# Gate and up products with head and rest of the tokens side by side in 512 columns, in a two-layer decoder trunk

## The chip, the core and the metric

The kernel runs on one core of a Trainium2 chip. The metric is the device time of one execution in microseconds, the median of three runs. The engines that matter: TensorE (PE in the profile), which multiplies and writes its sums into PSUM, eight banks of 512 fp32 columns in 128 partitions; VectorE (DVE) and ScalarE (ACT), which read PSUM and work on SBUF; SP and POOL (GpSimd), which issue the loads of the weights.

## The reference

Two residual layers on 512 tokens of 1024 features, in fp32. The first mixes tokens by causal pooling windows, the second by dilated sliding-window attention; after each mixer comes a SwiGLU feed-forward, and a last norm ends it. The change touches the feed-forward alone:

```python
D_FF = -(-8 * D_MODEL // (3 * 256)) * 256      # 2816
...
def swiglu(h, w_gate, w_up, w_down):
    g = jnp.einsum('bsd,df->bsf', h, w_gate)
    u = jnp.einsum('bsd,df->bsf', h, w_up)
    return jnp.einsum('bsf,fd->bsd', jax.nn.silu(g) * u, w_down)
...
    for i in range(DEPTH):
        ...
        h = rmsnorm(x, norm_ffn[i])
        x = x + swiglu(h, ffn_w_gate[i], ffn_w_up[i], ffn_w_down[i])
```

## The kernel before

**Heads and rests.** Every fp32 operand of a product is split into two parts: a head (`hi`, the value cast to the format fp32r, by ACT, line 139 for weights) and a rest (`lo`, value minus head, by DVE, line 143). A product is then three matmuls into one PSUM sum: head times head, weights' head times tokens' rest, weights' rest times tokens' head. Each matmul loads its own 128x128 stationary tile.

**Seven products for eight.** In the feed-forward the weights and tokens are cut into two-by-two blocks, and seven block products do the work of eight. Their operands are sums and differences of blocks; for the weights these are formed by loads that add (POOL, line 107) and by DVE (line 145), for the tokens before the first group.

**Groups.** `ffn` (line 537) works through 11 groups of 256 of the 2816 inner features. A group is seven products, `Group.product` (line 614), numbered 0 to 6. Each runs over gate and up (`g`), four chunks of 128 input features and the three matmuls (lines 623 to 628): 24 matmuls of 256 columns (half of the tokens) per product. The sums collect in three one-bank tensors: p takes products 0, 2, 4, 6, r takes 1 and 5, q takes 3. After each product `done` (line 632) reads them: `keep` is a copy of p after product 0 (line 636), `ct` gets copies of r and p after 1 and 2 (638, 640), then DVE sums after 3, 4, 5 (642, 644, 646), silu and the multiplication by up (647 to 650, 653 and 658). `first_half` and `second_half` build the seven token operands `u` of the down products and split them.

**Down.** After group 3, 6 and 9 a down stage (`down`, line 696) multiplies the `u` of three groups by seven combinations of the down weights: for each, two halves of 128 tokens, three groups, three matmuls of 512 columns (line 712), and after each half DVE adds the sum to or takes it from the stream x (719, 721). It uses p, r and q too, two banks of each; here q takes product 3 from zero, and product 0's p is added to x by itself. Groups 9 and 10 go through a last stage without the seven products.

**Order.** PE runs in program order (`manual_schedule`); the instructions of the other engines are ordered by the framework's scheduler, which obeys priorities: the readers of sums are marked `URGENT` (2000), those after products 5 and 6 have 100. The weights of all products stand in one list in the order of use (`FFN_ORDER`, line 47, filled by `enqueue_ffn`); `weights` (line 118) loads up to ten entries ahead and splits up to four ahead. A ring of five tiles holds split weights, another of five the raw ones, and three more (`vraw`) those that are formed by adding. The first weight's raw tile is kept until it has been added to the second's.

**PSUM.** Four banks belong to the pool `mm` (q, and other stages), four to `ffps` (two tensors each of p and r).

Of the kernel before, what the change touches and what calls it, by code (L numbers as in the profile page):

```python
# [17 lines left out]
P = 128  # L18
S = 512
# [27 lines left out]
FFN_ORDER = (  # L47
    [("two", 0)] + [("quad", n) for n in (2, 3)] + [("down", 0)]
    + [("quad", n) for n in (4, 5, 6)] + [("down", 1)] + [("quad", n) for n in (7, 8, 9)] + [("down", 2)]
    + [("quad", 10)] + [("last", 3)]  # L50
)

TWO = [(g, i) for g in (0, 1) for i in (0, 3)] + [(g, i) for i in (1, 2, 4, 5, 6) for g in (0, 1)]
# [5 lines left out]
def trunk_kernel(ctx: ExitStack, tc: tile.TileContext, x_in, xT, gam, gains, consts, ident_d, w0, wT, w1, wv, w_down, out):  # L59
# [15 lines left out]
    mm = ctx.enter_context(tc.tile_pool(name="mm", bufs=4, space=bass.MemoryType.PSUM))  # L75
# [92 lines left out]
    def enqueue_ffn(layer):  # L168
# [27 lines left out]
        def down(b):  # L196
            pairs = BLOCKS[b]
            at = layer * (NF // 2) + pairs[0]
            dn[b] = [{}, {}]
            for i in range(7):  # L200
                for js, a, n in zip(dn[b], (at, at + 2), (2, len(pairs) - 2)):
                    operand(js, i, lambda m, k: tiles[k, :, a : a + n, COLS[m]], (n, S), 10)

        for step, n in FFN_ORDER:
            if step == "two":
                for g, i in TWO:
                    quad(n + g, i, 5)
            elif step == "quad":
                for i in range(7):
                    quad(n, i)  # L210
            elif step == "down":
                down(n)
            else:
                dn[n] = [rows_of(w_down)(layer * NF + 2 * pair, half) for pair in BLOCKS[n] for half in range(2)]
# [27 lines left out]
    h_both = [stat.tile([P, NC * S + 2 * SHIFT], F32R, name=f"h_{part}") for part in ("hi", "lo")]  # L242

    def tokens_at(shift):
        return [h[:, shift : shift + NC * S].rearrange("p (c s) -> p c s", c=NC) for h in h_both]
# [291 lines left out]
    def ffn(layer, norm, third, nxt):  # L537
# [8 lines left out]
        with ExitStack() as fctx:  # L546
# [5 lines left out]
            fps = open_pool("ffps", 2, space=bass.MemoryType.PSUM)  # L552
            early_u = open_pool("ffa", 2)
            third_chain = norm.chain.ins
            h_hi, h_lo = tokens_at(SHIFT)
            block = lambda t, k, n: t[:, 4 * k : 4 * k + 4, HALVES[n]]

# [3 lines left out]
            t2, t3, t4 = ([fp.tile([P, 4, 256], F32R, name=f"t_{part}{i}") for part in ("hi", "lo")] for i in (2, 3, 4))  # L561
            fp.tile([P, SHIFT], F32, name="gap3")
            T_hi, T_lo = ([block(h, 0, 1), t2[i], t3[i], t4[i]] for i, h in enumerate((h_hi, h_lo)))
            RIGHT = (
                [(block(h_hi, 0, 0), block(h_lo, 0, 0))] + [(T_hi[i], T_lo[i]) for i in (0, 1)]
                + [(block(h_hi, 1, 0), block(h_lo, 1, 0)), (T_hi[2], T_lo[2])]
                + [(block(h_hi, 1, 1), block(h_lo, 1, 1)), (T_hi[3], T_lo[3])]
            )
# [12 lines left out]
            class Group:  # L581


                def __init__(self, n, ct):
                    self.n, self.ct, self.sums = n, ct, {}
                    self.lst = ct.rearrange("p m n g c -> p (m n g) c")
                    pool = early_u if n % 4 < 2 else late_u[0]
                    self.u = u_of[n] = [pool.tile([P, 7, 256], F32R, name=t) for t in ("u_hi", "u_lo")]

                def first_half(self):  # L590

                    (hi, lo), lst = self.u, self.lst
# [21 lines left out]
                def product(self, i):  # L614
                    if i == 3:
                        self.sums["q"] = mm.tile([P, S], F32, name="mm").rearrange("p (g c) -> p g c", g=2)
                    elif i < 2:
                        self.sums["pr"[i]] = fps.tile([P, 2, 256], F32, name="pr"[i])
                    ps = self.sums["prpqprp"[i]]
                    whi, wlo = weights(gu[self.n][i])  # L620
                    hi, lo = RIGHT[i]
                    for g in range(2):
                        for c in range(4):
                            for k, (w, xx) in enumerate(((whi, hi), (whi, lo), (wlo, hi))):
                                nc.tensor.matmul(  # L625
                                    ps[:, g, :], lhsT=w[:, g, c, :], rhs=xx[:, c, :],
                                    start=i in (0, 1, 3) and g + c + k == 0, stop=c == 3 and k == 2, skip_group_check=True,
                                )
                    with tc.high_priority(URGENT if i < 5 else 100):
                        self.done(i)  # L630

                def done(self, i):
# [12 lines left out]
                    elif i == 5:  # L645
                        nc.vector.tensor_add(ct[:, 0, 1], r, ct[:, 0, 1])
                        nc.scalar.activation(ct[:, 0, :, 0, :], ct[:, 0, :, 0, :], AF.Silu)
                        nc.vector.tensor_mul(ct[:, 0, :, 0, :], ct[:, 0, :, 0, :], ct[:, 0, :, 1, :])
                        nc.scalar.activation(ct[:, 1, 1, 0, :], ct[:, 1, 1, 0, :], AF.Silu)
                        nc.vector.tensor_mul(ct[:, 1, 1, 0, :], ct[:, 1, 1, 0, :], ct[:, 1, 1, 1, :])  # L650
                        self.first_half()
# [42 lines left out]
            r_tile = lambda: by_four(fps.tile([P, 2, 256], F32, name="r").rearrange("p g c -> p (g c)"))  # L694

            def down(b):

                pairs = BLOCKS[b]

                p, r = ([fps.tile([P, 2, 256], F32, name=t).rearrange("p g c -> p (g c)") for _ in range(2)] for t in "rp")  # L700
                q = [mm.tile([P, S], F32, name="mm") for _ in range(2)]
                where = (0, 1, 2, 3, 6, 5, 4)
# [544 lines left out]
```

## Time and profile before

| | |
|---|---|
| median of 3 runs | 1001.14 us (1000.97 to 1001.79) |
| the profiled execution | 1000.84 us |
| its span, first to last instruction | 999.0 us |
| TensorE matmuls | 6575 |
| VectorE, ScalarE busy | 784.6 us, 529.5 us |
| first feed-forward | about 113 to 447 us from the start |
| second feed-forward | about 661 us to the end |

In the rows of the timeline the first number is the start and the second the duration, both in microseconds; then engine, line, operation, output and inputs by name. In the grouped rows stand the count, the busy time in microseconds with the mean of one in nanoseconds, and the idle time of the engine before them with what ended it. Matmuls overlap: what one of them takes from the engine is the distance from its start to the next one's. The names p and r of down's tensors are exchanged in the profile against those in the code.

### The profile page before, as it was taken

What the parts mean: (1) busy time and instruction counts of PE and PEld (TensorE: products, weight loads), DVE (VectorE), ACT (ScalarE), POOL (GpSimd) and SP (SyncE); (2) the same over time, 40 slices, a digit from 0 to 9 for tenths busy, and PEclk for the clock granted to TensorE, in tenths of its full rate; (3) what the DMA queues carried; (4) which work ended last, traced back from release to release, by engine and by line L of the source; (5) the groups of instructions that cost most, each with busy time, mean ns of one, the idle gap of its engine ahead of it and who ended that gap; (6) DMA issues with size and microseconds to landing.
All of it is one profiled execution on the core that took longest, in us unless ns stands there. A gap on an engine that the chain in (4) does not pass through costs nothing.

```text
span 999.0 us, 16591 instructions
## 1 busy us (share of the span) xinstructions
PE 990.7 (99%) x6575; PEld 908.5 (91%) x6575; DVE 784.6 (79%) x1116; ACT 529.5 (53%) x838; POOL 113.1 (11%) x114
## 2 busy tenths in 40 slices
PE   9999999999999999999999999999999999999997
PEld 8888999989989998989888899899998998999896
DVE  6475799898888888777887557479989889788875
ACT  5573666545644554573543544356654554455354
POOL 0002010110011100002112024101011100111000
PEclk9999999999999999999999999999999999999999
DMA  9457277668559755524211249427666855975522
GB/s 334 177 168 190 60 197 177 151 187 233 149 126 292 182 137 148 183 76 135 83 58 53 62 153 284 92 64 196 174 158 200 234 148 123 289 179 138 155 67 84
DMA packets 76461, 157.29 MB, mean 157 GB/s; under 512 B 5904, under 2 KB 6288, under 8 KB 76384
## 3 DMA queue, kind: packets, MB, share of 16 engines
q1 hardware_dynamic: 58000, 121.00, 36.2%
q0 software_dynamic: 18096, 34.98, 20.3%
q8 instruction: 51, 0.84, 0.3%
q10 hardware_dynamic: 288, 0.27, 0.1%
q14 instruction: 26, 0.21, 0.1%
HBM read 154.08 MB, written 2.13 MB: 156 GB/s over the span
## 4 chain that ended last, share of the span: by engine, by line
PE 97%; ACT 1%; DMA 1%; DVE 1%; POOL 0%; issue 0%; DVEq 0%; ACTq 0%
PE p L625 25%; PE r L625 13%; PE r L712 10%; PE mm L625 6%; PE p L712 5%; PE mm L766 4%; PE mm L227 4%; PE mm L229 4%; PE mm L228 4%; PE mm L712 2%; PE early L443 2%; PE mm L363 2%; PE mm L361 2%; PE mm L362 2%; PE early L490 1%; PE tp L955 1%
## 5 line engine op out<-in xcount | busy, mean ns | idle before, releaser
L139 ACT CAST whi<-wraw 128x1024 fp32r<-128x1024 f32 (+2 forms) x189 | 184.9, 981 | 186.7 <-issue 45.8
L143 DVE TENSOR_TENSOR wlo<-wraw,whi 128x1024 fp32r<-128x1024 f32 (+2 forms) x190 | 221.1, 1165 | 76.2 <-ACT whi L139 75.7
L139 ACT CAST whi<-vraw 128x1024 fp32r<-128x1024 f32 (+1 forms) x102 | 99.6, 977 | 144.8 <-DVE vraw L145 53.7
L625 PE MATMUL p<-t_hi,wlo 128*128 128x256 f32 x528 | 149.8, 284 | 0.0
L625 PE MATMUL p<-t_lo,whi 128*128 128x256 f32 x528 | 149.4, 283 | 0.0
L625 PE MATMUL p<-t_hi,whi 128*128 128x256 f32 x528 | 148.4, 281 | 0.0
L143 DVE TENSOR_TENSOR wlo<-vraw,whi 128x1024 fp32r<-128x1024 f32 (+1 forms) x102 | 114.9, 1127 | 14.0 <-ACT whi L139 13.7
L625 PEld LDWEIGHTS p<-t_hi,whi 128*128 128x128 f32 x528 | 100.0, 189 | 0.0
L625 PE MATMUL r<-h_hi,wlo 128*128 128x256 f32 x352 | 99.9, 284 | 0.0
L625 PEld LDWEIGHTS p<-t_hi,wlo 128*128 128x128 f32 x528 | 99.6, 189 | 0.0
L625 PE MATMUL r<-h_lo,whi 128*128 128x256 f32 x352 | 99.6, 283 | 0.0
L625 PEld LDWEIGHTS p<-t_lo,whi 128*128 128x128 f32 x528 | 99.3, 188 | 0.0
L625 PE MATMUL r<-h_hi,whi 128*128 128x256 f32 x352 | 99.0, 281 | 0.0
L145 DVE TENSOR_TENSOR vraw<-vraw,wraw 128x1024 f32<-128x1024 f32 x68 | 76.6, 1127 | 0.8
L107 POOL DMA_DIRECT2D wraw<-w x22 | 26.7, 1211 | 435.6 <-DVE wlo L143 125.5
L625 PEld LDWEIGHTS r<-h_hi,whi 128*128 128x128 f32 x352 | 66.7, 189 | 0.0
L625 PEld LDWEIGHTS r<-h_hi,wlo 128*128 128x128 f32 x352 | 66.4, 189 | 0.0
L625 PEld LDWEIGHTS r<-h_lo,whi 128*128 128x128 f32 x352 | 66.2, 188 | 0.0
L227 PE MATMUL mm<-h_hi,whi 128*128 128x512 f32 (+1 forms) x176 | 64.8, 368 | 0.0
L229 PE MATMUL mm<-h_hi,wlo 128*128 128x512 f32 (+1 forms) x176 | 63.6, 361 | 0.0
L228 PE MATMUL mm<-h_lo,whi 128*128 128x512 f32 (+1 forms) x176 | 63.5, 361 | 0.0
L712 PE MATMUL r<-whi,u_lo 128*128 128x512 f32 x144 | 56.1, 390 | 0.0
(329 smaller groups left out, 2493.8 us busy)
## 6 DMA issues: line engine op xcount, KB each, us to landing
wraw<-w SPq DMA_DIRECT2D x116, 512.0 KB, 4.7
wraw<-w_down SPq DMA_DIRECT2D x32, 512.0 KB, 3.6
vraw<-w SPq DMA_DIRECT2D x22, 512.0 KB, 5.2
wraw<-w POOLq DMA_DIRECT2D x22, 512.0 KB, 7.6
vraw<-w POOLq DMA_DIRECT2D x22, 512.0 KB, 8.6
wraw<-wT SPq DMA_DIRECT2D x16, 512.0 KB, 4.4
wraw<-w_down SPq DMA_DIRECT2D x24, 256.0 KB, 2.7
vraw<-w_down SPq DMA_DIRECT2D x6, 512.0 KB, 5.5
```

The costliest lines, as they stand in the source:

```text
L107: nc.gpsimd.dma_start(dst, more, accum_op=ALU.add)
L139: nc.scalar.copy(hi[:, :n], raw[:, :n])
L143: nc.vector.tensor_sub(lo[:, :n], raw[:, :n], hi[:, :n].bitcast(F32))
L145: nc.vector.tensor_add(raws[into][:, :n], raws[into][:, :n], raws[more][:, :n])
L227: nc.tensor.matmul(ps, lhsT=whi, rhs=xhi, start=first, stop=False, **kw)
L228: nc.tensor.matmul(ps, lhsT=whi, rhs=xlo, start=False, stop=False, **kw)
L229: nc.tensor.matmul(ps, lhsT=wlo, rhs=xhi, start=False, stop=last, **kw)
L361: nc.tensor.matmul(ps, lhsT=xhi, rhs=w[0][:, k, :], start=first, stop=False)
L362: nc.tensor.matmul(ps, lhsT=xhi, rhs=w[1][:, k, :], start=False, stop=False)
L625: nc.tensor.matmul(ps[:, g, :], lhsT=w[:, g, c, :], rhs=xx[:, c, :], start=i in (0, 1, 3) and g + c + k == 0, stop=c == 3 and k == 2, skip ...
L712: nc.tensor.matmul(acc[t], lhsT=u, rhs=w, start=i in (0, 1, 3) and c + k == 0, stop=c == len(pairs) - 1 and k == 2, skip_group_check=True,)
L766: nc.tensor.matmul(ps, lhsT=u, rhs=w[:, m, :], start=z + m + k == 0, stop=z == 1 and m == 1 and k == 2,)
```

## The change

**Side by side.** The head and rest of the tokens become two planes of one tensor (`h`, and `t2` to `t4` for the sums of blocks), at the same places in SBUF as before. For groups 3 to 9 of each layer, called paired, products 0, 2, 3, 5 and 6 run eight matmuls of 512 columns (the weights' head on the tokens' head and rest, the result in two halves of one bank) and then eight of 256 (weights' rest on tokens' head, added to the first half, `own`). Products 1 and 4 remain 24 matmuls of 256, into one half. Groups 0, 1, 2 and 10 stay as they were.

**Two-bank tensors.** From the end of group 1 to group 10 PSUM is four tensors of two banks: A twice (used in turn by group and down), Q and C. A has one bank for gate and one for up. Since the two halves have to be added anyway, the sums that two results share are continued instead of begun anew: ACT copies A into Q after product 0, and product 3 adds to Q; ACT copies A into C after product 2, and products 1 and 5 add to C. The halves are added when read: ACT copies the second half (`more`) to `ct`, DVE adds the first.

**Down** uses A for products 0, 2, 4, 6, C for 1 and 5, Q for 3. Its first sum is copied from A to Q by ACT, product 3 adds to it, and both reach x together. DVE adds 1024 columns at a time, after both halves of the tokens.

**Order.** Product 0 of a paired group is put ahead of products 5 and 6 of the group before; then follow 2, 3, 1, 4. The down stage begins with its product 0 ahead of 5 and 6 of the group, and product 0 of the next group stands ahead of the down's last product. The list of weights follows, except that a group's weights 1 to 4 stay in that order, since 2 is formed from 1; `held` counts the ring for that. The tensors `u` are opened when they are first written.

```diff
+BODY, USED = (1, 2, 3, 4), (2, 3, 1, 4)
+PAIRED = range(3, 10)
+
+def _plan():
+    first = lambda n: [("quad", n, 0)] if n in PAIRED else []
+    steps = TWO + [("one", 2, i) for i in range(6)] + first(3) + [("one", 2, 6)]
+    for n in PAIRED:
+        steps += [("quad", n, i) for i in USED]
+        ends = [("quad", n, 5), ("quad", n, 6)]
+        if n % 3 == 0:
+            b = n // 3 - 1
+            steps += [("down", b, 0)] + ends + [("down", b, i) for i in range(1, 6)] + first(n + 1) + [("down", b, 6)]
+        else:
+            steps += first(n + 1) + ends
+    return steps + [("one", 10, i) for i in range(7)] + [("last", 3, 0)]
...
-    h_both = [stat.tile([P, NC * S + 2 * SHIFT], F32R, name=f"h_{part}") for part in ("hi", "lo")]
+    h_both = stat.tile([P, 2, NC * S + 2 * SHIFT], F32R, name="h")
...
+                def product(self, i, held=0):
+                    whi, wlo = weights(gu[self.n][i], held=held)
+                    right = RIGHT[i]
+                    if self.pairs:
+                        a, q, c = self.pairs
+                        to = (a, c, a, q, a, c, a)[i]
+                        places = [(g, k) for g in range(2) for k in range(4)]
+                        mat = lambda o, w, m, **kw: nc.tensor.matmul(o, lhsT=w, rhs=m, skip_group_check=True, **kw)
+                        own = lambda g: to[:, g, HALVES[i == 1]]
+                        if i in (1, 4):
+                            for g, k in places:
+                                mat(own(g), whi[:, g, k, :], right[:, 0, k, :], start=False, stop=False)
+                                mat(own(g), whi[:, g, k, :], right[:, 1, k, :], start=False, stop=False)
+                                mat(own(g), wlo[:, g, k, :], right[:, 0, k, :], start=False, stop=k == 3)
+                        else:
+                            for g, k in places:
+                                both = to[:, g, :].rearrange("p (z c) -> p z c", z=2)
+                                mat(both, whi[:, g, k, :], right[:, :, k, :], start=i == 0 and k == 0, stop=False)
+                            for g, k in places:
+                                mat(own(g), wlo[:, g, k, :], right[:, 0, k, :], start=False, stop=k == 3)
+                        with tc.high_priority(URGENT if i < 5 else 100):
+                            self.paired_done(i)
+                        return
...
+                def paired_done(self, i):
+                    ct = self.ct
+                    a, q, c = self.pairs
+                    own, more = HALVES
+                    if i == 0:
+                        nc.scalar.copy(q, a)
+                    elif i == 2:
+                        nc.scalar.copy(c, a)
+                    elif i == 3:
+                        nc.scalar.copy(ct[:, 0, 0], q[:, :, more])
+                        nc.vector.tensor_add(ct[:, 0, 0], q[:, :, own], ct[:, 0, 0])
+                    elif i == 1:
+                        nc.scalar.copy(ct[:, 1, 1], c[:, :, more])
+                    elif i == 4:
+                        nc.vector.scalar_tensor_tensor(
+                            ct[:, 1, 1], a[:, :, own], -1.0, ct[:, 1, 1], op0=ALU.mult, op1=ALU.subtract
+                        )
+                    elif i == 5:
+                        nc.scalar.copy(ct[:, 0, 1], c[:, :, more])
+                        nc.vector.tensor_add(ct[:, 0, 1], c[:, :, own], ct[:, 0, 1])
+                        self.gate_first()
+                    elif i == 6:
+                        nc.scalar.copy(ct[:, 1, 0], a[:, :, more])
+                        nc.vector.scalar_tensor_tensor(
+                            ct[:, 1, 0], a[:, :, own], -1.0, ct[:, 1, 0], op0=ALU.mult, op1=ALU.subtract
+                        )
+                        nc.scalar.activation(ct[:, 1, 0, 0, :], ct[:, 1, 0, 0, :], AF.Silu)
+                        nc.vector.tensor_mul(ct[:, 1, 0, 0, :], ct[:, 1, 0, 0, :], ct[:, 1, 0, 1, :])
+                        self.second_half()
...
+            class Down:
...
+                    self.b, self.accs, self.p, self.q = b, (p, r, p, q, p, r, p), p, q
...
-                                    acc[t], lhsT=u, rhs=w, start=i in (0, 1, 3) and c + k == 0,
+                                    acc[:, t, :], lhsT=u, rhs=w, start=i in (0, 1) and c + k == 0,
...
+                    with tc.high_priority(URGENT):
+                        to = x[:, 2 * n : 2 * n + 2, COLS[half]]
+                        if i == 0:
+                            nc.scalar.copy(self.q, acc)
+                        elif sign > 0:
+                            nc.vector.tensor_add(to, acc, to)
+                        else:
+                            nc.vector.tensor_sub(to, to, acc)
...
+                groups[n].product(i, held={1: -2, 2: 1, 3: 1}.get(i, 0) if kind == "quad" else 0)
+                if (n, i) == (1, 6):
                     held.close()
                     late_u.append(open_pool("ffb", 2))
...
+                    fps.close()
+                    mm.close()
+                    fps.open("ffpairs", [P, 2, S], 1)
+                    *A, Q, C = (fps.tile(f"pair{i}") for i in range(4))
+                    A.reverse()
```

More of the change, by code (lines that the diff above doesn't have):

```diff
@@ L46 @@
 BLOCKS = ((0, 1, 2), (3, 4, 5), (6, 7, 8), (9, 10))
[L47 to L53, printed above, removed]
+TWO = [("one", g, i) for g in (0, 1) for i in (0, 3)] + [("one", g, i) for i in (1, 2, 4, 5, 6) for g in (0, 1)]
+BODY, USED = (1, 2, 3, 4), (2, 3, 1, 4)
[12 more added lines that the diff above has]
+    return steps + [("one", 10, i) for i in range(7)] + [("last", 3, 0)]
+PLAN = _plan()
 TOKENS = np.arange(S).reshape(J, R).T.reshape(-1)
@@ L194, in enqueue_ffn, with down @@
         tiles = w_down.rearrange("(n k p) c -> k p n c", k=2, p=P)
-        def down(b):
+        def down(b, i):
             pairs = BLOCKS[b]
             at = layer * (NF // 2) + pairs[0]
[L199 to L209, printed above, removed]
+            for js, a, n in zip(dn.setdefault(b, [{}, {}]), (at, at + 2), (2, len(pairs) - 2)):
+                operand(js, i, lambda m, k: tiles[k, :, a : a + n, COLS[m]], (n, S), 10)
+        for kind, n, i in PLAN:
+            if kind == "one":
+                quad(n, i, 5 if n < 2 else 10)
+            elif kind == "quad":
+                if i == USED[0]:
+                    for each in BODY:
+                        quad(n, each)
+                elif i not in BODY:
                     quad(n, i)
-            elif step == "down":
-                down(n)
+            elif kind == "down":
+                down(n, i)
             else:
@@ L617, in product @@
                     elif i < 2:
-                        self.sums["pr"[i]] = fps.tile([P, 2, 256], F32, name="pr"[i])
+                        self.sums["pr"[i]] = by_g(fps.tile("pr"[i]))
                     ps = self.sums["prpqprp"[i]]
-                    whi, wlo = weights(gu[self.n][i])
-                    hi, lo = RIGHT[i]
                     for g in range(2):
                         for c in range(4):
-                            for k, (w, xx) in enumerate(((whi, hi), (whi, lo), (wlo, hi))):
+                            for k, (w, z) in enumerate(((whi, 0), (whi, 1), (wlo, 0))):
@@ new lines, in ffn @@
+            groups = {0: Group(0, ct_common), 1: Group(1, ct_tile(hn, "ct_second"))}
+            downs = {}
+            with tc.issue_after(third_chain):
+                first_tokens(0, t1r)
+                first_tokens(1, b21r)
+            for at, (kind, n, i) in enumerate(PLAN[:-1]):
+                if at in (0, 2):
+                    b = 2 + at // 2
+                    if b == 2:
+                        late_banks[b] = third
+                        norm.prepare(3, COLS)
+                    else:
+                        late_banks[b] = [r_tile(), by_four(mm.tile())]
+                        for half in range(2):
+                            norm.turn(b, half, late_banks[b][half])
+                    late(b, 1)
+                if at in (4, 6, 8):
+                    for b in (2, 3):
+                        late(b, at // 2)
+                if kind == "down":
+                    if i == 0:
+                        downs[n] = Down(n, A[0], C, Q)
+                        A.reverse()
+                    downs[n].product(i)
+                    continue
+                if kind == "quad" and i == 0:
+                    groups[n] = Group(n, ct_common, (A[0], Q, C))
+                    A.reverse()
+                elif i == 0 and n not in groups:
+                    if n == 10:
+                        fps.close()
+                        mm.open()
+                        fps.open("ffps", [P, S], 2)
+                    groups[n] = Group(n, ct_common)
+                groups[n].product(i, held={1: -2, 2: 1, 3: 1}.get(i, 0) if kind == "quad" else 0)
+                if (n, i) == (1, 6):
@@ L744, in ffn @@
                     held.close()
                     late_u.append(open_pool("ffb", 2))
[L746 to L751 removed]
+                    fps.close()
+                    mm.close()
+                    fps.open("ffpairs", [P, 2, S], 1)
+                    *A, Q, C = (fps.tile(f"pair{i}") for i in range(4))
```

127 lines of the change are left out of this document (61 added, 66 removed).

## The prediction

> **What bounds the kernel now.** I read the page first, its busy line, its clock line and its chain.
>
> ```profile
> PE 990.7 (99%) x6575; PEld 908.5 (91%) x6575; DVE 784.6 (79%) x1116; ACT 529.5 (53%) x838; POOL 113.1 (11%) x114
> ...
> PEclk9999999999999999999999999999999999999999
> ...
> PE 97%; ACT 1%; DMA 1%; DVE 1%; POOL 0%; issue 0%; DVEq 0%; ACTq 0%
> PE p L625 25%; PE r L625 13%; PE r L712 10%; PE mm L625 6%; PE p L712 5%; PE mm L766 4%; PE mm L227 4%; PE mm L229 4%; PE mm L228 4%; PE mm L712 2%; PE early L443 2%; PE mm L363 2%; PE mm L361 2%; PE mm L362 2%; PE early L490 1%; PE tp L955 1%
> ```
>
> The chain is TensorE (PE) almost throughout, at full granted clock, and its largest parts are the gate and up products (L625: 25, 13 and 6%). A busy PE need not be at its peak, so next I took the busy times by stage: the first feed-forward as a whole, then, inside it, three groups (230 to 291 us) and one down stage (291 to 319 us).
>
> ```profile
> 113.00:447.00 334.00, 334.00 (x2368) 314.86 (x2367) 285.18 (x369) 188.58 (x255) 32.95 (x29) 1.00 0.63 169
> ...
> 230.00:291.00 61.00, 61.00 (x486) 59.92 (x485) 50.41 (x63) 34.60 (x45) 7.80 (x7) 1.00 0.70 179
> 291.00:319.00 28.00, 28.00 (x147) 24.12 (x146) 25.55 (x31) 12.97 (x15) 3.59 (x3) 1.00 0.75 204
> ```
>
> Columns: length, busy time of PE, weight load, VectorE (DVE), ScalarE (ACT) and POOL, clock, DMA share, GB/s. PE has no gap in 334 us. DVE is at 83% in the groups and 91% in the down stage, ACT at 57% and 46%. So time can fall only by giving PE less to do, and rise only by making it wait. What one matmul costs PE is its distance to the next one, not the 280 ns printed as its duration; so last I took the timeline of PE and read where products begin.
>
> ```profile
> 319.21 0.28 PE L625 MATMUL p<-t_hi,whi 128*128 128x256 f32 x1
> ...
> 322.09 0.28 PE L625 MATMUL mm<-h_hi,whi 128*128 128x256 f32 x1
> ...
> 301.22 0.39 PE L712 MATMUL r<-whi,u_hi 128*128 128x512 f32 x1
> ...
> 305.30 0.39 PE L712 MATMUL p<-whi,u_hi 128*128 128x512 f32 x1
> ```
>
> The first pair bounds one gate-and-up product: 24 matmuls of 256 columns in 2.88 us, 120.0 ns each. The second pair bounds one down product, 18 matmuls of 512 columns in 4.08 us, 226.7 ns each. Twice the columns cost 106.7 ns more, so a matmul costs 0.417 ns a column and 13.3 ns whatever its width.
>
> **PE's work.** Per weight tile a product had whi on head, whi on rest, wlo on head: 3 x 120.0 = 360 ns. Now five of the seven products (0, 2, 3, 5, 6) have whi on both in one of 512, and wlo on head: 226.7 + 120.0 = 346.7 ns. That saves 13.3 ns in each of 8 tiles, 5 products, 7 groups, 2 layers: 560 x 13.3 = 7.5 us. Products 1 and 4 stay at 2.88 us; the merged ones take 8 x 346.7 = 2.77 us. Not shown by those rows is a moving operand in two runs that lie far apart (head and rest). The nearest rows are L227 to L229 at the start of attention, whose 256 columns are read, and written, in four runs of 64:
>
> ```profile
> 447.54 0.28 PE L227 MATMUL mm<-h_hi,whi 128*128 128x256 f32 x1
> ...
> 450.42 0.28 PE L227 MATMUL mm<-h_hi,whi 128*128 128x256 f32 x1
> ```
>
> 24 matmuls in 2.88 us again, so runs cost nothing that can be seen. I bound the saving by 0 (each run pays 13.3 ns of its own) and 13.3 ns a pair, and take 13.3, from these rows.
>
> The Trainium skill, TensorE: Matmul & The Clock Gate, section "Wait — 56ns, not 53.3ns?", gives a warm matmul its columns at 2.4 GHz plus only about 2.5 ns. By that figure, as an estimate, the merging would save 560 x 2.5 = 1.4 us, about nothing; the slope of the rows above agrees with it, the fixed part does not, and I go by the rows.
>
> **ACT and DVE.** The head's and rest's sums now lie side by side and are added when read.
>
> ```profile
> L139 ACT CAST whi<-wraw 128x1024 fp32r<-128x1024 f32 x156 | 163.6, 1051 | 130.8 <-issue 32.3 <-PE p L625 20.5 <-PE mm L228 17.8
> L636 ACT COPY keep<-p 128x512 f32<-128x512 f32 x22 | 12.8, 582 | 3.9 <-PE p L625 3.9
> L644 DVE SCALAR_TENSOR_TENSOR ct<-p,ct 128x512 f32<-128x512 f32 x20 | 13.7, 687 | 11.4 <-PE p L625 11.4
> L658 DVE SCALAR_TENSOR_TENSOR ct<-p,ct 128x256 f32<-128x256 f32 x20 | 8.4, 418 | 0.0
> L719 DVE TENSOR_TENSOR x<-r,x 128x512 f32<-128x512 f32 x24 | 16.5, 686 | 0.0
> L145 DVE TENSOR_TENSOR vraw<-vraw,wraw 128x1024 f32<-128x1024 f32 x56 | 68.3, 1220 | 0.6
> ```
>
> ACT in a group: the copies after products 0 and 2 grow to 1024 columns between PSUM banks, which no row shows; the cast of 1024 (1.05 us) and twice 582 ns (1.16) bound one, I take 1.1, so +0.5 us each. Three more copies of 512, after products 3, 5 and 6, are +0.58 each. Together 2.8 us, x 14 groups = 39 us; the six copies of a down's first sum add 6.6. ACT goes from 529.5 to 575 us. DVE: after product 6 a 512 sum (0.69) stands beside the 256 product that was there, +0.69 x 14 = 9.6 us; in a down 14 adds of 512 (9.6 us) become six of 1024 (7.3 us, priced by L145), -2.3 x 6 = -13.7. DVE stays at about 780 of 993 us. Neither becomes the bound: they lie beside PE, whose cover is the 61 of 61 and 28 of 28 us above; an exposed 1.1 us copy would cost its full length.
>
> **Places where PE can now wait.** Each sum has one tensor, so three hand-overs have a deadline.
>
> (a) C after product 5 of a group that precedes a down: the down's product 1 begins in C one product (2.77 us) later, and first ACT must copy the rest's half and DVE add the head's. Six places. In the trace product 5 ends at 281.97 and the down starts at 284.85:
>
> ```profile
> 281.97 0.28 PE L625 MATMUL p<-t_hi,whi 128*128 128x256 f32 x1
> 282.05 0.62 ACT L139 CAST whi<-vraw 128x512 fp32r<-128x512 f32 x1 [1.51 <-PE r L625]
> 281.74 1.22 DVE L145 TENSOR_TENSOR vraw<-vraw,wraw 128x1024 f32<-128x1024 f32 x1
> 282.87 0.68 DVE L646 TENSOR_TENSOR ct<-r,ct 128x512 f32<-128x512 f32 x1
> ...
> 284.85 0.39 PE L712 MATMUL r<-whi,u_hi 128*128 128x512 f32 x1
> ```
>
> Behind that cast the copy ends at 282.67 + 0.58 = 283.25 and the add at 283.9, 2.0 us after the product; with one more DVE operation of 1.22 ahead, 3.2. So 0 to 0.4 us each, 0 to 2.6 in all. Queued behind the add on DVE is the low part of the next weights, which has products of slack.
>
> (b) C is filled from A after product 2 and used by product 1, with product 3 (2.77 us) between; 14 places. The row it is like is the copy after product 2:
>
> ```profile
> 253.17 0.28 PE L625 MATMUL mm<-h_hi,whi 128*128 128x256 f32 x1
> 253.25 1.05 ACT L139 CAST whi<-wraw 128x1024 fp32r<-128x1024 f32 x1 [0.59 <-PE p L625]
> 254.21 0.58 ACT L640 COPY ct<-p 128x512 f32<-128x512 f32 x1
> ```
>
> Product 2 ends at 253.17, a cast slips in, the copy starts 1.04 us after; at 1.1 us it would end at 2.1 to 2.2, 0.6 before the deadline. I take 0.
>
> (c) After a down, the next group begins with product 2, so both the first and second weights of its body must be split, the second after an addition to the first. Four places. In the trace the down's sixth product ends at 309.38:
>
> ```profile
> 309.38 0.39 PE L712 MATMUL r<-whi,u_hi 128*128 128x512 f32 x1
> 309.58 0.69 DVE L719 TENSOR_TENSOR x<-p,x 128x512 f32<-128x512 f32 x1 [1.08 <-PE p L712]
> 310.19 1.22 DVE L143 TENSOR_TENSOR wlo<-vraw,whi 128x1024 fp32r<-128x1024 f32 x1
> 311.44 1.23 DVE L145 TENSOR_TENSOR vraw<-vraw,wraw 128x1024 f32<-128x1024 f32 x1
> ...
> 314.26 1.22 DVE L143 TENSOR_TENSOR wlo<-vraw,whi 128x1024 fp32r<-128x1024 f32 x1
> ```
>
> They are split (310.19, 314.26) by 315.48, 6.1 us after that product. The new order leaves product 0 of the next group and the down's last, 2.77 + 4.08 = 6.85 us; the wider add after the sixth product takes 0.5 of the margin. Wait 0; with one DVE operation more in the way, 1.2 us x 4 = 4.9.
>
> Weights of the down's own products are its tightest cover already:
>
> ```profile
> 296.19 0.69 DVE L143 TENSOR_TENSOR wlo<-wraw,whi 128x512 fp32r<-128x512 f32 x1
> ...
> 297.14 0.39 PE L712 MATMUL mm<-whi,u_hi 128*128 128x512 f32 x1
> ```
>
> 0.26 us from 296.88 to 297.14, and this one is the product's second tile, used six matmuls (1.4 us) later. DVE has less to do in a down than before, so I put nothing there. The new loading order keeps the transfers of SP's and POOL's queues in number and size. Product 0 of the next group moves ahead of 5 and 6 of this one, so its load (SP) comes before theirs (SP and POOL), and its raw tile, one of five, is held for two or three splits more until it is added to product 1's weights. With 25 to 30% of the DMA time free in the rows by stage I price this at nothing; if a load came late for it, it would be (c)'s wait.
>
> **The sum.** The profiled execution took 1000.84 us (span 999.0 and 1.8 around it); the median of the runs shown is 1001.14, 0.3 more. 1000.84 - 7.5 + 0.6 (a part of (a)) = 993.9, on the median 994.2. With all bounds at their ends it is 993.6 to 1001.1.
>
> **Rivals.**
>
> Half kept: (a) and (c) at their upper bounds, 2.6 + 4.9 = 7.5, would eat all; one of them in most places leaves 996 to 999.1. For it: only 0.4 to 0.9 us of slack. Against: at all such places PE waited for nothing before. 0.17.
>
> No gain: the merged matmul costs two fixed parts, or the waits sum to about the saving: 999.1 to 1003.1. For it: no row has runs so far apart. Against: the four-run rows. 0.11, of which 0.03 is a fixed part of only 2.5 ns, 1001.1 - 1.4 = 999.7. The page named above gives that figure.
>
> Slower: the copy in (b) is queued on ACT behind the cast u_hi of the group before, which itself waits for a longer DVE chain.
>
> ```profile
> 244.53 0.28 PE L625 MATMUL p<-h_hi,whi 128*128 128x256 f32 x1
> ...
> 248.50 0.58 ACT L636 COPY keep<-p 128x512 f32<-128x512 f32 x1
> 249.19 1.27 ACT L320 CAST u_hi<-ct 128x1280 fp32r<-128x1280 f32 x1
> ```
>
> Product 6 ended at 244.53, the cast at 250.46; a copy behind it ends 7.0 us after product 6, where products 2 and 3 allow 5.5. That is 1.5 us x 14 = 21 us: 993.7 + 21 = 1014.7. It decides from (7.5 + 2.0) / 14 = 0.7 us a group. Against it: here the urgent copy went ahead of that cast. 0.09.
>
> **How the numbers follow.** My case (993.2 to 996) has 0.63, half kept 0.17, no gain 0.11, slower 0.09. The time is that of my case, 994.2. The range 993.2 to 999.5 takes the first two and a little of the third, 0.8; its low end is the full saving and half a microsecond of scatter. Faster by over 0.2% (2.0 us, about what a measurement of this kernel tells from no change) is the first two: 0.80; within 0.2% 0.11; slower 0.09.
>
> **What the profile after should show.** Matmuls of 512 columns in gate and up 226.7 ns apart, merged products of 2.77 us; some 6015 matmuls; no wait of PE on ACT or DVE in the list of waits; ACT near 575 us, DVE near 780. I am wrong if the distance is near 240 ns, if PE lists waits for an ACT copy into Q or C or for a DVE add from C, or if gaps stand ahead of a down's product or the first product after it.

## The result, and the profile after

The changed kernel takes 1008.56 us (median of 4 runs, 1007.38 to 1009.39), the kernel before in the same session 1001.06 (1000.79 to 1001.79). The ratio is 1.0073, with a 95% interval of 1.0055 to 1.0090: slower by 7.5 us, where the forecast was faster by 6.9. The profiled execution took 1008.86 us, its span is 1007.1.

From the page of the changed kernel, the busy line, TensorE's slices and its clock:

```profile
PE 990.0 (98%) x6015; PEld 882.0 (88%) x6015; DVE 782.7 (78%) x1082; ACT 562.4 (56%) x886; POOL 113.0 (11%) x114
...
PE   9999998999999999999999999999899999999997
...
PEclk9999999999999999999999999999899999999999
```

The 560 matmuls are gone (6575 before, 6015 now), and DVE (782.7 us) and ACT (562.4 us) are near the 780 and 575 that were expected. But TensorE's row has an 8 in two slices, from 151 to 176 and from 705 to 730 us, one in each layer. The list of PE's waits has a first row that was not there before (columns: total us, times, longest):

```profile
PE pair L694 <- ACT keep L743: 8.2, 2, 4.1
```

L694 is the ordinary product, L743 the copy `keep` after product 0. So the wait is in a group that is *not* paired. It is group 2, the first to write into the new two-bank tensors: there its product 0 goes into one bank of A. PE's timeline of the changed kernel at that place:

```profile
161.35 0.28 PE L694 MATMUL pair<-h,wlo 128*128 128x256 f32 x1
165.73 0.50 PE L694 MATMUL pair<-t,whi 128*128 128x256 f32 x2 [4.10 <-ACT keep L743]
...
167.41 0.63 PE L694 MATMUL pair<-t,whi 128*128 128x256 f32 x2
167.83 0.41 PE L694 MATMUL pair<-t,wlo 128*128 128x256 f32 x1
168.05 0.63 PE L694 MATMUL pair<-t,whi 128*128 128x256 f32 x2
```

Product 1 ends at about 161.5, product 2 of the group starts at 165.73. It adds to the sum of product 0, so it may not start before that sum has been copied. Why was the copy late? ACT's timeline of the changed kernel, and then the same stretch of the kernel before:

```profile
157.37 1.26 ACT L351 CAST u_hi<-ct 128x1280 fp32r<-128x1280 f32 x1
158.53 0.37 ACT L756 ACTIVATE ct_second<-p 128x256 f32<-128x256 f32 x1
162.99 1.26 ACT L351 CAST u_hi<-ct_second 128x1280 fp32r<-128x1280 f32 x1 [4.08 <-DVE ct_second L656]
164.15 1.04 ACT L166 CAST whi<-vraw 128x1024 fp32r<-128x1024 f32 x1
165.10 0.58 ACT L743 COPY keep<-pair 128x512 f32<-128x512 f32 x1
```

```profile
157.52 1.26 ACT L320 CAST u_hi<-ct 128x1280 fp32r<-128x1280 f32 x1
158.69 0.37 ACT L653 ACTIVATE ct_second<-p 128x256 f32<-128x256 f32 x1
158.96 0.59 ACT L636 COPY keep<-p 128x512 f32<-128x512 f32 x1
...
163.17 1.27 ACT L320 CAST u_hi<-ct_second 128x1280 fp32r<-128x1280 f32 x1
```

Before, `keep` was copied at 158.96, and the cast of group 1's `u` came at 163.17, when DVE had its input ready. After, the cast stands first in ACT's order. ACT takes its instructions in order, so it stands idle for 4.08 us until DVE has formed `ct_second`, then casts `u` and a weight, and only then copies. Nothing that the cast needs has changed; only the order has.

The wait isn't all. In the rows of PE above, from 167.41 to 168.05 three matmuls of 256 columns take 0.64 us, 213 ns each, against 120.0 otherwise. The busy times by stretch show why (columns as in the prediction: length, PE, weight load, DVE, ACT, POOL, clock, DMA share, GB/s):

```profile
160.00:166.00 6.00, 1.90 (x16) 1.69 (x15) 4.68 (x6) 3.01 (x4) 1.21 (x1) 1.00 0.59 184
166.00:172.00 6.00, 6.00 (x39) 6.00 (x39) 2.67 (x3) 2.64 (x4) 0.88 (x1) 0.72 0.61 126
172.00:178.00 6.00, 6.00 (x52) 6.00 (x51) 4.43 (x6) 2.23 (x3) 0.00 (x0) 1.00 0.47 94
...
717.00:723.00 6.00, 5.79 (x28) 5.79 (x29) 2.52 (x3) 2.07 (x4) 0.69 (x1) 0.53 0.64 131
```

After the standstill the granted clock is 0.72 in the first layer and 0.53 in the second, each for one stretch, and then full again.

Where the 8.1 us between the two spans (999.0 and 1007.1) come from, by the starts of the products on PE, both layers together:

| stage | before | after | difference |
|---|---|---|---|
| group 2 | 39.9 us | 52.7 us | +12.8: 8.5 of standstill, 4.3 of slower products after it |
| groups 3 to 9, gate and up | 281.8 us | 276.4 us | -5.4 |
| a down product | 4.085 us | 4.093 us | +0.3 for all |
| attention and the rest | | | +0.4 |

The merged products themselves, from PE's timeline of the changed kernel:

```profile
249.86 2.02 PE L668 MATMUL pair<-t,whi 128*128 128x512 f32 x8
251.71 1.11 PE L668 MATMUL pair<-t,wlo 128*128 128x256 f32 x8
252.66 2.03 PE L668 MATMUL pair<-t,whi 128*128 128x512 f32 x8
254.52 1.12 PE L668 MATMUL pair<-t,wlo 128*128 128x256 f32 x8
255.48 2.02 PE L668 MATMUL pair<-h,whi 128*128 128x512 f32 x8
```

Two products from 249.86 to 255.48 are 2.81 us each, where 2.77 was forecast and 2.88 was the price before. Eight of 512 columns take 1.85 to 1.86 us, 232 ns each; eight of 256 take 0.95 to 0.96, 119 ns each.

### The profile page after: what moved, and what is told of

Read it like the earlier page. It is cut to its first block, busy times and chain, and to the rows that moved or that the text cites. A ratio compares the mean times of both kernels' runs of the same rounds, so it can differ in the third digit from the quotient of the medians.

```text
span 1007.1 us, 15515 instructions
## 1 busy us (share of the span) xinstructions
PE 990.0 (98%) x6015; PEld 882.0 (88%) x6015; DVE 782.7 (78%) x1082; ACT 562.4 (56%) x886; POOL 113.0 (11%) x114
## 4 chain that ended last, share of the span: by engine, by line
PE 92%; DVE 4%; ACT 2%; DMA 1%; issue 1%; POOL 0%; SPq 0%; ACTq 0%; DVEq 0%
PE pair L668 27%; PE pair L817 17%; PE p L694 6%; PE mm L887 4%; PE mm L254 4%; PE mm L256 4%; PE mm L255 4%; PE pair L694 3%; PE r L694 3%; PE mm L394 2%; PE mm L392 2%; PE mm L393 2%; PE mm L694 2%; PE early L474 2%; DVE wlo L170 1%
## 5 line engine op out<-in xcount | busy, mean ns | idle before, releaser
L668 PE MATMUL pair<-h,whi 128*128 128x512 f32 (+1 forms) x560 | 125.5, 349 | 0.0
L668 PEld LDWEIGHTS pair<-h,whi 128*128 128x128 f32 x560 | 95.4, 188 | 11.8
L817 PE MATMUL pair<-whi,u_lo 128*128 128x512 f32 x252 | 98.2, 390 | 0.0
L817 PE MATMUL pair<-wlo,u_hi 128*128 128x512 f32 x252 | 98.2, 390 | 0.0
L817 PE MATMUL pair<-whi,u_hi 128*128 128x512 f32 x252 | 98.1, 389 | 0.0
L668 PE MATMUL pair<-t,whi 128*128 128x512 f32 (+1 forms) x448 | 97.1, 338 | 0.0
L668 PEld LDWEIGHTS pair<-t,whi 128*128 128x128 f32 x448 | 74.8, 188 | 7.7
L668 PE MATMUL pair<-h,wlo 128*128 128x256 f32 x448 | 78.2, 281 | 0.0
L668 PEld LDWEIGHTS pair<-h,wlo 128*128 128x128 f32 x448 | 66.8, 188 | 3.9
L254 PE MATMUL mm<-h,whi 128*128 128x512 f32 (+1 forms) x176 | 64.8, 368 | 0.0
L256 PE MATMUL mm<-h,wlo 128*128 128x512 f32 (+1 forms) x176 | 63.6, 361 | 0.0
L255 PE MATMUL mm<-h,whi 128*128 128x512 f32 (+1 forms) x176 | 63.5, 361 | 0.0
```

The lines of the kernel that those rows point to most:

```text
L254: nc.tensor.matmul(ps, lhsT=whi, rhs=xhi, start=first, stop=False, **kw)
L255: nc.tensor.matmul(ps, lhsT=whi, rhs=xlo, start=False, stop=False, **kw)
L256: nc.tensor.matmul(ps, lhsT=wlo, rhs=xhi, start=False, stop=last, **kw)
L668: mat = lambda o, w, m, **kw: nc.tensor.matmul(o, lhsT=w, rhs=m, skip_group_check=True, **kw)
L817: nc.tensor.matmul(acc[:, t, :], lhsT=u, rhs=w, start=i in (0, 1) and c + k == 0, stop=c == len(pairs) - 1 and k == 2, skip_group_check=True,)
```

## The experiments

Two questions were left. First, what makes group 2 wait, and does the wait explain the slower clock after it? I set *order* (the copy is only late in ACT's order) against *bank* (the new tensors themselves make the wait). Second, why is a merged product 2.81 us? There *pace* (matmuls here have another fixed part than I derived) stood against *runs* (the operand in two far-apart runs costs time). The kernels e1 to e4 ran beside the kernel before at 1000.75 us, e5 to e8 beside it at 1000.68, e9 and e10 beside it at 1000.82.

**e1: the copy first.** The split of group 1's last five `u` is held back and issued in group 2, ordered behind the copy `keep`. Two SBUF pools, `held` and `ffb`, are therefore closed and opened after product 0 of group 2 instead of ahead of it; the PSUM tensors are opened where they were.

```diff
-                    split(hi[:, 2:7, :], lo[:, 2:7, :], lst[:, 3:8, :])
+                    rest = lambda: split(hi[:, 2:7, :], lo[:, 2:7, :], lst[:, 3:8, :])
+                    if self.n == 1:
+                        waiting.append(rest)
+                    else:
+                        rest()
...
-                        nc.scalar.copy(keep, p)
+                        kept = nc.scalar.copy(keep, p)
+                        if self.n == 2:
+                            with tc.issue_after(kept.ins), tc.high_priority(100):
+                                waiting.pop()()
...
-                if (n, i) == (1, 6):
+                if (n, i) == (2, 0):
                     held.close()
                     late_u.append(open_pool("ffb", 2))
+                if (n, i) == (1, 6):
                     fps.close()
                     mm.close()
```

> Order theory: the loss is one wait per layer, 4.1 us each, in which TensorE stands before product 2 of group 2 because ScalarE does the copy of the sum of product 0 (keep) behind a cast of group 1 (u_hi, 1280 columns) that itself waits 4.1 us for VectorE; with the slower matmuls after it this group takes 6.0 and 6.9 us more than before in the two layers. With the copy issued ahead of that cast the wait goes and the time falls by about 12.8 us, to 995.8 us, 0.5% under the kernel before. Bank theory (rival): TensorE waits because the new two-bank tensors lie on banks of groups 0 and 1 that are read late; then the order of two ScalarE instructions changes nothing, and the time stays at 1007 to 1009.

Measured: 995.51 us (995.09 to 995.95), ratio to before 0.9945 (0.9933 to 0.9958). ACT's timeline of e1, and one stretch of its busy times:

```profile
160.11 0.57 ACT L747 COPY keep<-pair 128x512 f32<-128x512 f32 x1
162.28 1.27 ACT L351 CAST u_hi<-ct_second 128x1280 fp32r<-128x1280 f32 x1 [1.60 <-DVE ct_second L656]
```

```profile
166.00:172.00 6.00, 6.00 (x52) 6.00 (x52) 5.39 (x7) 2.83 (x4) 0.88 (x1) 1.00 0.94 174
```

The copy is back ahead of the cast, PE has 6.00 of 6.00 us at clock 1.00, and the list of waits no longer has a row for `keep`. The two-bank tensors are the same as in the changed kernel, so *bank* falls. The order on ACT was worth about 13 us (1008.56 - 995.51), and without the late copy the change is faster than the kernel before. That it is the order, and not the moved SBUF pools, is borne out by e7 below, which turns the order round without moving any pool.

**e2: one run.** e1, with the merged matmuls reading 512 columns that lie side by side, by a new helper `one_run` (its lines are left out here). The columns are those of other tokens, so the kernel's sums are not the reference's.

```diff
-                                mat(both, whi[:, g, k, :], right[:, :, k, :], start=i == 0 and k == 0, stop=False)
+                                mat(both, whi[:, g, k, :], one_run(i, k), start=i == 0 and k == 0, stop=False)
```

> As the kernel with the copy first, but the merged matmuls read 512 columns that lie in one piece, not 256 of the heads and 256 of the rests; the sums are thus those of other tokens. Run theory: a moving operand in two runs costs 6 ns (232.5 ns to the next matmul measured, 226.7 in the rows of 512 of before), so a merged product falls from 2.81 to 2.77 us and the time by 70 x 0.036 = 2.5 us. Pace theory (rival): the distance is set by the weight loads or the mixture of widths, and the products stay at 2.81 us, the time within 0.5 us of the kernel with the copy first.

Measured: 995.79 us, ratio 0.9948 (0.9935 to 0.9962). The merged products are 2.808 us in both. PE's timeline of e2:

```profile
249.67 1.79 PE L679 MATMUL pair<-h,whi 128*128 128x512 f32 x7
251.30 1.10 PE L679 MATMUL pair<-h,wlo 128*128 128x256 f32 x8
```

Seven matmuls in 1.63 us (249.67 to 251.30) are 233 ns each, as with two runs. *Runs* falls.

**e3: unmerged.** e1, each matmul of 512 again two of 256, all else of the change kept.

```diff
-                                mat(both, whi[:, g, k, :], right[:, :, k, :], start=i == 0 and k == 0, stop=False)
+                                for z in range(2):
+                                    mat(both[:, z], whi[:, g, k, :], right[:, z, k, :], start=i == 0 and k + z == 0, stop=False)
```

> As the kernel with the copy first, but each merged matmul of 512 columns is again two of 256, each with its own weight load; order, tensors and copies stay. It measures what the merging alone is worth. By the rows of products 1 and 4 after the change (2.85 us) the 70 products take 0.041 us more each: 2.9 us more than with the copy first. By the rows of before (2.88 us) 0.071 each: 5.0 us more. By the fixed part of 13.3 ns a matmul that the prediction took: 7.5 us more.

Measured: 1001.59 us, ratio 1.0008 (0.9999 to 1.0017); the products are 2.875 us. So merging by itself is worth 1001.59 - 995.51 = 6.1 us, where 7.5 was forecast, and all the rest of the change (copies, two-bank tensors, order), with the wait taken out, costs between -0.1 and +1.7 us.

**e4: filled.** The changed kernel with 18 matmuls of 512 columns, whose result nobody reads, into the second bank of the tensor ahead of the late product, to keep PE busy through the wait.

```diff
+                if (n, i) == (2, 2):
+                    for _ in range(18):
+                        nc.tensor.matmul(
+                            A[1][:, 1, :], lhsT=h_hi[:, 0, :P], rhs=h_hi[:, 0, :], start=True, stop=True, skip_group_check=True
+                        )
```

> The changed kernel with 18 matmuls of 512 columns (4.1 us) into a bank that group 2 does not use, put before its product 2, so that TensorE works where it waited. Clock theory: of the 12.8 us that group 2 takes more in both layers, 8.5 are the wait and 4.3 come from matmuls at a lower granted clock after it; with TensorE busy the clock stays and the time falls by about 4 us, to 1004.5. Rival: those matmuls are slow for another reason (late weights, late reads of sums), and the time stays at 1008.6.

Measured: 1017.62 us, ratio 1.0167 (1.0151 to 1.0183). A miss: PE's waits in e4 say that the fillers (L866) themselves waited, though they write the bank that the copy doesn't read.

```profile
PE pair L866 <- ACT keep L743: 8.2, 2, 4.1
```

So the dependency is taken for the whole two-bank tensor. The standstill stayed and the fillers came on top of it, so this tells nothing of the clock.

**e6: filled, elsewhere.** As e4, with the fillers in the other A, which is free then (`A[0][:, 1, :]` for `A[1][:, 1, :]`).

> The changed kernel with 18 matmuls of 512 columns put before product 2 of group 2 again, now into the tensor that the next group will use, so that they need not wait for the copy themselves. Clock theory: they fill the 4.1 us of the wait, the clock stays at 1.00, the matmuls after it keep 118 to 120 ns, and of the 12.8 us that group 2 costs in both layers only the waits remain, 8.5: 995.5 + 8.5 = 1004.0 us. Rival: the matmuls after the wait are slow for another reason, and the time stays at 1008.6.

Measured: 1004.69 us, ratio 1.0043 (1.0028 to 1.0058). From the busy times of e6:

```profile
160.00:166.00 6.00, 5.98 (x34) 4.93 (x33) 4.67 (x6) 3.13 (x4) 1.21 (x1) 1.00 0.66 183
166.00:172.00 6.00, 6.00 (x53) 6.00 (x52) 3.55 (x4) 3.03 (x5) 0.00 (x0) 1.00 0.60 127
```

ACT's order is that of the changed kernel and the copy as late, but PE worked through, and the clock stays at 1.00. 1008.56 - 1004.69 = 3.9 us is what the two standstills cost beyond their length.

**e7: the copy late.** The kernel *before*, with one edit: in group 2 the copy `keep` is ordered behind group 1's cast of `u`.

```diff
-                    split(hi[:, 2:7, :], lo[:, 2:7, :], lst[:, 3:8, :])
+                    if self.n == 1:
+                        late_hi.append(nc.scalar.copy(hi[:, 2:7, :], lst[:, 3:8, :]))
+                        nc.vector.tensor_sub(lo[:, 2:7, :], lst[:, 3:8, :], hi[:, 2:7, :].bitcast(F32))
...
-                        nc.scalar.copy(keep, p)
+                        with tc.issue_after(late_hi[0].ins) if self.n == 2 else nullcontext():
+                            nc.scalar.copy(keep, p)
```

> The kernel before, with one edge: in group 2 the copy of product 0's sum is issued behind the cast u_hi of group 1. Order theory: this alone brings the loss, without any of the new tensors: about 4 us of waiting in each layer and slower matmuls after it, 12.8 us in all, 1013.6 us. Rival: the wait hurts only with the new tensors; then the time stays within 2 us of 1000.8.

Measured: 1011.49 us (1009.01 to 1012.23), ratio 1.0104 (1.0091 to 1.0118). ACT's timeline and PE's wait in e7:

```profile
163.04 1.26 ACT L613 CAST u_hi<-ct_second 128x1280 fp32r<-128x1280 f32 x1
164.20 0.59 ACT L641 COPY keep<-p 128x512 f32<-128x512 f32 x1
```

```profile
PE p L629 <- ACT keep L641: 6.4, 2, 3.2
```

The order alone, without anything else of the change, brings 10.8 us. That is below the 12.8 expected because the copy follows the cast at once (164.20, against 165.10 with a weight's cast between) and the waits are 3.2 us each, not 4.1.

**e8: a later switch.** The changed kernel, group 2 left in the old tensors; the two-bank tensors are opened after its product 6, and product 0 of group 3 follows.

```diff
-    steps = TWO + [("one", 2, i) for i in range(6)] + first(3) + [("one", 2, 6)]
+    steps = TWO + [("one", 2, i) for i in range(7)] + first(3)
...
-                    if self.n == 2 and i in (0, 1, 3):
-                        self.sums["prqq"[i]] = by_g({0: A[1], 1: C, 3: Q}[i][:, 0, :])
-                    elif i == 3:
+                    if i == 3:
...
+                if (n, i) == (2, 6):
                     fps.close()
```

> The changed kernel with the switch to two-bank tensors after group 2 instead of before it; group 2 uses the old tensors, and product 0 of group 3 follows product 6 of group 2. The copy keep of group 2 then stands ahead of the cast of group 1, as before the change, but the first copy from a new tensor (A to Q, group 3) stands behind the cast u_hi of group 2. Switch theory: what comes late is the first read of a tensor opened at the switch, wherever it lies; the 4 us wait goes from product 2 of group 2 and appears at product 2 of group 3, and the time is 1006 to 1010. Rival: the late copy belongs to group 2 alone; the time is 996 to 999.

Measured: 1007.21 us (1006.08 to 1009.3), ratio 1.0068 (1.0055 to 1.0082). PE's wait and ACT's timeline in e8:

```profile
PE pair L668 <- ACT pair L704: 7.9, 2, 4.0
```

```profile
179.86 1.26 ACT L351 CAST u_hi<-ct 128x1280 fp32r<-128x1280 f32 x1 [1.17 <-DVE ct L656]
181.03 1.01 ACT L704 COPY pair<-pair 128x1024 f32<-128x1024 f32 x1
```

`keep` is early again, and now the first read of a new tensor, the copy of A into Q after group 3's product 0 (L704), stands behind group 2's cast of `u` and makes PE wait 4.0 us. The wait goes with the place where the tensors are opened, not with group 2. In both cases the copy that reads a tensor for the first time after the switch stands behind the cast. That the opening is the reason is inferred from these two places, not shown: only in e8 does product 0 of a paired group follow directly on product 6 of the group before, so no run has the same order of products with tensors that were opened long before. By which rule the scheduler put the copy there the traces don't tell; priorities are the same, and I leave that open.

**e5: taking turns.** e1, with the matmuls of 512 and 256 columns of one weight tile in turn instead of eight and eight (one loop for both instead of two). It asks if the order of widths sets the pace.

> As the kernel with the copy first, but in a merged product the matmul of 512 columns and the one of 256 with the same weight tile follow one another, in place of eight and then eight. Order-of-widths theory: the merged product's 2.81 us come from runs of equal matmuls, whose distances scatter (224 to 241 ns); in alternation they are 226.7 and 120.0 as in the rows of before, a product takes 2.77 us, and the time falls by 70 x 0.036 = 2.5 us, to 993.0 us. Rival: the distances of 512 columns are 232.5 ns in any order here; the time stays within 0.5 us of 995.5.

Measured: 996.34 us, ratio 0.9957 (0.9945 to 0.9970); merged products 2.805 us, as in e1. The order of widths doesn't matter for them. That e5 is 0.8 us slower than e1 comes from products 1 and 4, which take 2.88 us here and 2.85 in e1; why is open.

**e9 and e10: 512 columns throughout.** e1 with the weights' rest multiplied by the tokens' rest as well, so that all 16 matmuls of a merged product have 512 columns; in e9 eight and eight, in e10 in turn.

```diff
-                                mat(own(g), wlo[:, g, k, :], right[:, 0, k, :], start=False, stop=k == 3)
+                                both = to[:, g, :].rearrange("p (z c) -> p z c", z=2)
+                                mat(both, wlo[:, g, k, :], right[:, :, k, :], start=False, stop=k == 3)
```

> In e1 a merged product's matmuls of 512 columns stand about 232.5 ns apart, where the down's own stand 226.7 ns apart. Here every matmul of a merged product has 512 columns: the low part of the weights is multiplied with the rests too, in the same order (eight of the high part, eight of the low part, by tiles), so the gate and up sums are not the reference's. Theory mixture (a 512 loses time because 256s stand beside it): 16 x 226.7 = 3.63 us a product. Theory place (the 512s of gate and up are slower by themselves): 16 x 232.5 = 3.72 us a product.

> As e9, with the high and the low part's matmuls of one tile taking turns, which is the order of the down product, so that each right operand is used twice in a row. Theory mixture: 3.63 us a product, as e9. Theory operand (a 512 is quicker where its right operand was just read): 3.63 us here and 3.72 us in e9. Theory place: 3.72 us in both.

Measured: 1059.63 and 1059.52 us (one run each). PE's timeline of e9, two products and then a down product to its end:

```profile
253.05 2.02 PE L672 MATMUL pair<-t,whi 128*128 128x512 f32 x8
254.91 2.02 PE L672 MATMUL pair<-t,wlo 128*128 128x512 f32 x8
...
260.49 1.79 PE L672 MATMUL pair<-h,whi 128*128 128x512 f32 x7
...
329.95 0.39 PE L825 MATMUL pair<-whi,u_hi 128*128 128x512 f32 x1
...
333.82 0.39 PE L825 MATMUL pair<-whi,u_lo 128*128 128x512 f32 x1
334.05 2.02 PE L672 MATMUL pair<-t,whi 128*128 128x512 f32 x8
```

From 253.05 to 260.49, 32 matmuls take 232.5 ns each, 3.72 us a product; the down product beside them, 18 from 329.95 to 334.05, takes 227.8. In e10:

```profile
249.77 0.40 PE L672 MATMUL pair<-h,whi 128*128 128x512 f32 x1
...
253.73 0.39 PE L672 MATMUL pair<-t,wlo 128*128 128x512 f32 x1
```

17 distances in 3.96 us, 233 ns. *Mixture* and *operand* fall, *place* holds: a matmul of 512 columns takes some 5 ns more in gate and up than in down, whatever width stands next to it.

What it is about the place stays open. The two stages differ in that gate and up hold weights stationary and stream tokens, down the reverse, but this alone isn't it. The attention's projections (L254 to L256) hold weights stationary and stream 512 tokens too. PE's timeline of the changed kernel there:

```profile
480.81 0.39 PE L254 MATMUL mm<-h,whi 128*128 128x512 f32 x1
...
483.53 0.39 PE L254 MATMUL mm<-h,whi 128*128 128x512 f32 x1
```

These are 12 matmuls in 2.72 us, 226.7 ns each, as in down. One difference was not tried. In the projections and in down the head's stationary tile is used for two matmuls in a row (head, head, rest); in the merged products, and in e9 and e10, every matmul has another tile than the one before. The expectation of e10 calls its order that of the down product, but it repeats the streamed operand, where down repeats the stationary one.

## Why the prediction was wrong

**The step that failed** is the list under "Places where PE can now wait". It named three hand-overs, all within paired groups and downs, and for each of them it was right: no wait of PE appears at (a), (b) or (c). It left out group 2, in which the tensors change, though its seven products and their copies are those of before. The copy after its product 0 reads a tensor that is new from there on, and it lost its place in ACT's order: 165.10 us instead of 158.96, behind the cast. The deadline there is one product, 2.85 us, and the cast ahead waits 4.08 us for DVE. This order accounts for the 13 us between the changed kernel and e1, and put into the kernel before it costs 10.8 (e7). Why the order turned is not shown.

**The mechanism of the "slower" rival came true at another place.** It said: an urgent copy queued behind the cast `u_hi`, which waits for DVE. It put this at 14 places at 1.5 us each and gave it 0.09, since in the trace of before "the urgent copy went ahead of that cast". That row showed what the scheduler had chosen for the old tensors, and I used it as if it held for the new. At the 14 places PE waits for nothing; at two others the order turned, with a standstill of 4.3 us each.

**The clock was not in any term.** A standstill was priced at its own length. Here each wait of 4.1 us cost about 2 us more through the clock (e6: 3.9 for two). The Trainium skill, TensorE: Matmul & The Clock Gate, section "What's actually happening", says that the clock is halved after an idle window of about 3.4 us, and full again after a busy one. The trace agrees in the halving (a granted clock of 0.51 in a row of e7 below, and after the wait 213 ns for 256 columns against 120.0); how long a standstill must be is another matter, below.

**PE's work was mis-sized.** The fixed part of 13.3 ns came from a 512 of the down stage and a 256 of gate and up. In gate and up a 512 takes 232.5 ns, so two of 256 exceed it by 2 x 120.0 - 232.5 = 7.5 ns, not 13.3: 560 x 7.5 = 4.2 us. The matmuls of 256 in the paired groups came out at 119 instead of 120.0, which for 560 + 672 of them brought about another 1.2. By the starts of products in the traces of e3 and e1, the merged products became 4.8 us shorter in sum and products 1 and 4 0.7; that is 5.5 of the 6.1 us between their times. Why the 256s became shorter is open. The other end of that bound, two runs costing a second fixed part, is ruled out by e2.

**A sum was added up wrongly.** "With all bounds at their ends" the time was to be 993.6 to 1001.1. But with the stated bounds, a saving of 0 and waits of 2.6 and 4.9, the upper end is 1001.1 + 7.5 = 1008.6 us. That the measured time is almost this is chance: the saving was there, and neither of the two waits was.

**What was right.** 6015 matmuls. ACT was to be near 575 us and is at 562.4; a copy of 1024 columns between banks takes 1.01 us in e8, not 1.1. DVE is at 782.7, near 780. Neither bounds the kernel. With the one order mended, e1 takes 995.51 us, 1.3 above the forecast and about the 1.4 by which the merging was over-priced. That this fits so closely is in part luck: hand-over (a) was given 0.6 us and costs nothing visible, while the downs and group 2 take some 0.3 us more each, in sum, than before. So the sum came near for the paired groups, and failed at the way into them.

## What to carry to other kernels

When a change opens new tensors, follow the first reader of each of them through the in-order queue of its engine: an order that the trace of before shows was chosen for the old tensors and need not hold for the new. Price a standstill of TensorE of some 4 us at its length and, by the table and e6, about half as much again, and derive a matmul's fixed part from rows of the stage in which it will run. A cast that can wait long for another engine belongs, by an explicit order, behind every copy with a near deadline.

## What was not expected of the hardware

- The same matmul of 512 columns takes 232.5 ns in gate and up and 226.7 to 227.8 in down and in the attention's projections, also where all matmuls around it are of that width (e9).
- A moving operand in two runs, head and rest of the tokens far apart, costs nothing against one run (2.808 us a product in both, e2).
- Matmuls without a reader, put in the gap, keep the clock at 1.00 and make the kernel 3.9 us faster (e6), unless they write to a tensor that is waited for, where they stand in the wait themselves (e4).
- The clock can fall after the engine has gone on, or within the standstill. PE's timeline of e7, in the second layer:

```profile
715.57 0.28 PE L629 MATMUL r<-h_hi,wlo 128*128 128x256 f32 x1
719.04 0.39 PE L629 MATMUL p<-t_hi,whi 128*128 128x256 f32 x1 [3.19 <-ACT keep L641]
...
720.21 0.28 PE L629 MATMUL p<-t_hi,whi 128*128 128x256 f32 x1
...
720.47 0.41 PE L629 MATMUL p<-t_hi,wlo 128*128 128x256 f32 x1
720.68 0.41 PE L629 MATMUL p<-t_hi,whi 128*128 128x256 f32 x1
...
723.85 0.28 PE L629 MATMUL mm<-h_hi,whi 128*128 128x256 f32 x1
```

From 719.04 the matmuls run at full pace for 1.3 us, and only then, from 720.4 to 723.7, at 213 ns each. In the first layer of the same run, PE's last matmul ahead of the wait ends its turn at 161.5 and the next starts at 164.84. There the clock fell within the standstill (columns as above, the clock is the third from the end):

```profile
163.00:164.00 1.00, 0.00 (x0) 0.00 (x0) 1.00 (x1) 1.00 (x2) 0.00 (x0) 1.00 0.35 49
164.00:165.00 1.00, 0.16 (x1) 0.16 (x1) 1.00 (x2) 0.79 (x2) 0.44 (x1) 0.51 0.76 293
```

That is 2.5 us after the last matmul's turn. The slow stretch in the second layer, 3.3 us, has about the length of the window in the Trainium skill, TensorE: Matmul & The Clock Gate, section "What's actually happening". But the last 3.4 us ahead of it hold 1.3 us of matmuls, and those ahead of 164.0 in the first layer hold 0.9, so in neither place was a whole window idle. Here that section and the rows differ, and the rows decide: standstills of 3.35 us (715.69 to 719.04 and 161.49 to 164.84) were enough.
